# Second layer of a two-layer encoder: the softmax weights transposed by VectorE in 32x32 blocks and a trip through DRAM, in place of TensorE transposes

## The chip, the cores and the metric

The kernel runs on one core of a Trainium2 chip. The metric is the device time of one execution in microseconds; the kernel before ran three times, 1224.99, 1226.17 and 1229.44 us, median 1226.17. A core has five engines with a queue of instructions each, taken in order: TensorE (PE, matmuls; its weight loads are shown apart as PEld), VectorE (DVE), ScalarE (ACT), GpSimd (POOL) and SyncE (SP), which here issues nearly all DMAs. SBUF holds the working data, PSUM the results of matmuls.

## The reference, cut to what matters

x is 1024 positions of 1024 features, the memory 256 rows. Layer 0 has windowed and dense grouped-query attention, layer 1 differential attention (C: 6 heads of 64, value width 128); both have a cross-attention (X: 4 heads) into the memory, a SiLU gate, and an output projection that is added to x. Layer 1, which alone the change touches:

```python
def odd_layer(x, mem_n, table, norm_g, w_in, lq1, lk1, lq2, lk2, subln_g, w_mem_kv, w_out, lam_init):
    h = rmsnorm(x, norm_g)
    q1, q2, k1, k2, v, xq, gate = _split(h @ w_in, ODD_SPLITS)
    ...
    s = jnp.einsum("ibqhd,ibshd->ibhqs", qi, kk) * (D ** -0.5)         # i: the two maps
    p = jax.nn.softmax(s + rel_bias_lookup(table, rel)[None, None], axis=-1)
    w = p[0] - lam * p[1]
    y_c = jnp.einsum("bhqs,bshe->bqhe", w, v)                          # per block of 128 queries
    y_c = rmsnorm(y_c, subln_g) * (1.0 - lam_init)
    y_x = memory_cross_attention(xq, mem_n, w_mem_kv)
    y = jnp.concatenate([y_c, y_x], axis=-1) * jax.nn.silu(gate)
    return x + y @ w_out
```

## The kernel before

All matmuls take their data as fp32r, a rounded form of fp32. Where the precision is needed, a value is held as two such numbers, hi (the rounded value) and lo (what the rounding left), and a product is a sum of two or three products of these. To "split" is to make hi by a copy on ScalarE and lo by a subtraction.

**Steps.** Attention goes in steps, one for a head (or, in X, for all four heads) and a block of 128 queries: in layer 1 8 steps of X (steps 0 to 7) and 48 of C (steps 8 to 55, eight for each head). `run_steps` (L475) runs them as a software pipeline. In its round i it emits, in this order: `hop` of step i-1, `s1` of step i, projection products as filler (`jobs.pull`), `s3` (value product) of a pair of steps that is ready, `s2` (transposes and split) of the step 2 before, `finish` of step i, and more filler. The filler is the projections of the coming heads (`acc`, L329) or, late in the layer, the early part of the output projection (`pre`); `po` is its rest. The order that the program text gives is not the final one: a list scheduler in the framework places each engine's instructions when the program is built, by its own estimates, and the order of each engine's queue is then fixed. `tc.issue_after(x)` keeps an instruction behind x; `keep_in_program_order` (used by the change) pins a DMA in SP's queue where the text has it.

**One step of C.** `s1`: for the two maps the scores `sc` of 128 queries by 1024 keys in PSUM, one after the other product with the keys' hi part (L1505, four matmuls of 128x512) and lo part (L1514, four). VectorE then adds the position bias and takes the row minimum in one pass per map (L1520: `e` from `sc` and `toep`), and ScalarE takes the exp in place and its row sum (L1523). `finish`: two small VectorE operations (L1528, L1530) and the combine of the two maps into one weight matrix `e` (L1532). `hop`: `word_copy`, a DMA of `e` to `er`, SBUF to SBUF, 512 KB, which only changes its type. `s2` (`dense_s2`, L570): eight TensorE transposes of 128x128 into PSUM (`te`, L580), four a bank, and from each bank the split into `PT` (`split_to`: hi on ScalarE L347, lo on VectorE L348). In C, `finish` of step i is kept behind the split of step i-2 (`behind`). `s3`, for two steps at once and one round after their last split: the value product `oc` (L1545, L1547: 16 matmuls), then the normalisation (`ssqc`, `rbcc`) and the gate.

**One step of X** is alike with other shapes: scores `sx` (L543), minimum, exp, a scaling on ScalarE in `finish`, the same hop and `s2`, and the value product `ox` (L656).

**Rings.** PSUM has two places of 128x1024 (`ps_s`: `sc`, `sx` and `ox` in turn), two of 128x512 for `te` and other small results (`ps_t`), and two for `acc`, `pre` and `oc` (`ps_a`). `e` has 4 buffers, `er` 2 in layer 1, `PT` one per half. Weights of the projections come by DMA (`wr`), are cast by VectorE (`wh`, L241), and their lo part is subtracted on GpSimd (`wl`, L243); output weights likewise (`wos`, L270 and L271).

## Time and profile before

| | |
|---|---|
| time of the runs | 1224.99, 1226.17, 1229.44 us, median 1226.17 |
| span of the profiled execution | 1228.9 us, 2.7 above that median; no other time of that execution is given |
| mean granted TensorE clock | 0.996 |
| layer 1, first scores of X to last value product of C | about 640 to 1157 us |
| busy in one head of C (741 to 820 us): PE, DVE, ACT, POOL | 79.0, 55.1, 38.8, 23.7 of 79 us |
| DMA in the same stretch | share 0.48 of 16 engines, 154 GB/s |
| last scores of C; last value product ends; output projection begins | 1135.9; 1157.3; 1162.0 us |
| HBM | 87.7 MB read, 39.9 MB written |

How to read it: the profile names each instruction by the line of the program that made it, its engine, its output and inputs. Busy time of TensorE is counted from the start of a matmul to its modelled end, and matmuls overlap, so the mean time of one (0.40 us for 128x512) is longer than the distance of two that follow each other (0.23 us). An order of instructions that is quoted below is the built program's, without any time; names carry buffer numbers there, and what stands in brackets are the engines whose semaphores an instruction waits for (DMAHW: a DMA).

### The profile page before, as it was taken

To read this page: it belongs to the slowest core of one execution; us is meant where nothing else is said; L and a number is where in the kernel's file an instruction comes from. 1 tells how busy PE (TensorE), PEld (TensorE's weight loads), DVE (VectorE), ACT (ScalarE), POOL (GpSimd) and SP (SyncE) were. 2 spreads that over 40 slices of the span, in tenths; PEclk is the share of its full clock that TensorE was granted. 3 is DMA by queue.
4 is the path that set the end of the run, shared out by engine and by line. 5 is a ranking of instruction groups with operands and counts; after the bars stand their busy time and mean duration, and the time that the engine had idled before them with its cause. 6 is when DMAs were issued, how large, how long until landed. Compare 5 with 4: busy or idle time off the path is not lost.

```text
span 1228.9 us, 19560 instructions
## 1 busy us (share of the span) xinstructions
PE 1196.5 (97%) x6614; PEld 988.4 (80%) x6614; DVE 801.1 (65%) x1495; ACT 663.1 (54%) x1477; POOL 436.3 (36%) x414
## 2 busy tenths in 40 slices
PE   6999999999999999999999999999999999999997
PEld 5788888888888777888888777777787777777886
DVE  5547665377778878635365866766767767667544
ACT  6248754366667766636157744555545454445332
POOL 5023365366665455437112222333143231301100
PEclk9999999999999999999999999999999999999999
DMA  6664445545465565457645445355363452468354
GB/s 257 200 194 147 163 172 163 166 160 207 163 233 209 208 227 191 151 196 237 186 158 156 153 146 164 121 183 163 124 187 125 153 171 105 149 212 285 121 192 155
DMA packets 114304, 216.70 MB, mean 176 GB/s; under 512 B 13302, under 2 KB 47478, under 8 KB 114204
## 3 DMA queue, kind: packets, MB, share of 16 engines
q1 hardware_dynamic: 114060, 215.25, 52.5%
q8 instruction: 53, 0.87, 0.3%
q14 instruction: 47, 0.39, 0.1%
q10 hardware_dynamic: 144, 0.20, 0.0%
HBM read 87.71 MB, written 39.86 MB: 104 GB/s over the span
## 4 chain that ended last, share of the span: by engine, by line
PE 47%; DVE 2%; DMA 1%; issue 1%; ACT 1%; POOL 0%; POOLq 0%; SPq 0%; DVEq 0%; ACTq 0%
PE acc L329 24%; PE po L702 5%; PE oc L1545 3%; PE sc L1505 3%; PE te L580 3%; PE sc L1514 2%; PE pre L702 2%; PE oc L1547 2%; DMA wr<-in_w_in 1%; PE ssqc L1563 1%; PE ox L656 0%; PE rbcc L1576 0%; PE tv L439 0%; PE sx L543 0%; DVE e L1520 0%
## 5 line engine op out<-in xcount | busy, mean ns | idle before, releaser
L329 PE MATMUL acc<-h,wh 128*128 128x512 f32 x1536 | 499.5, 398 | 1.6 <-DVE h L351 0.8
L329 PEld LDWEIGHTS acc<-h,wh 128*128 128x128 f32 x1536 | 282.4, 188 | 65.7 <-issue 7.9
L329 PE MATMUL acc<-h,wl 128*128 128x512 f32 x768 | 303.8, 396 | 1.5 <-POOL wl L243 1.2
L243 POOL TENSOR_TENSOR wl<-wr,wh 128x512 fp32r<-128x512 f32 x94 | 124.8, 1329 | 286.3 <-DVE wh L241 155.0
L1523 ACT ACTIVATE e<-e,mn 128x1024 f32<-128x1024 f32 x96 | 110.0, 1148 | 117.0 <-DVE mn L1520 116.9
L329 PEld LDWEIGHTS acc<-h,wl 128*128 128x128 f32 x768 | 144.3, 188 | 34.9 <-issue 4.4
L1114 POOL TENSOR_TENSOR e<-e,rz 128x1024 f32<-128x1024 f32 x48 | 91.6, 1910 | 84.2 <-DVE rz L1113 57.8
L1520 DVE CUSTOM_DVE_ANT_0 e<-sc,toep 128x1024 f32<-128x1024 f32 x96 | 113.5, 1218 | 8.0 <-PE sc L1514 7.3
L580 PEld LDWEIGHTS te<-identr,er 128*128 128x128 f32 x896 | 92.2, 143 | 18.8 <-PE sa L543 2.2
L580 PE MATMUL te<-identr,er 128*128 128x128 f32 x896 | 99.9, 246 | 4.3 <-DVE O L1578 1.4
L348 DVE TENSOR_TENSOR PT<-te,PT 128x512 fp32r<-128x512 f32 x112 | 74.3, 687 | 42.8 <-ACT PT L347 39.2
L241 DVE CAST wh<-wr 128x512 fp32r<-128x512 f32 x112 | 58.2, 522 | 42.9 <-PE acc L329 17.3
L348 DVE TENSOR_TENSOR PTl<-te,PTh 128x512 fp32r<-128x512 f32 x112 | 74.0, 684 | 9.4 <-ACT PTh L347 8.9
L1545 PE MATMUL oc<-PT,v 128*128 128x512 f32 x192 | 69.8, 403 | 0.7 <-DVE ckl L1420 0.7
L1532 DVE SCALAR_TENSOR_TENSOR e<-e,mr 128x1024 f32<-128x1024 f32 x48 | 66.3, 1381 | 1.5
L347 ACT CAST PT<-te 128x512 fp32r<-128x512 f32 x112 | 62.7, 589 | 7.2 <-PE te L580 6.7
L347 ACT CAST PTh<-te 128x512 fp32r<-128x512 f32 x112 | 62.2, 586 | 7.9 <-PE te L580 7.1
L702 PE MATMUL po<-woh,yh 128*128 128x512 f32 (+1 forms) x172 | 65.7, 382 | 0.0
L702 PE MATMUL po<-woh,yl 128*128 128x512 f32 (+1 forms) x172 | 65.5, 381 | 0.0
L702 PE MATMUL po<-wol,yh 128*128 128x512 f32 (+1 forms) x172 | 65.3, 380 | 0.0
L1105 DVE TENSOR_REDUCE mn<-sb 128x1 f32<-128x1024 f32 x48 | 58.3, 1216 | 7.0 <-PE sb L543 6.6
L350 ACT ACTIVATE yh<-yr 128x256 fp32r<-128x256 f32 (+2 forms) x56 | 24.0, 447 | 66.2 <-DMA yr<-ysc 37.5
(211 smaller groups left out, 2358.7 us busy)
## 6 DMA issues: line engine op xcount, KB each, us to landing
er<-e SPq DMA_DIRECT2D x112, 512.0 KB, 3.0
wr<-in_w_in SPq DMA_DIRECT2D x96, 256.0 KB, 3.0
ysc<-gy SPq DMA_DIRECT2D x16, 512.0 KB, 2.7
cq<-sg SPq DMA_DIRECT2D x64, 128.0 KB, 2.5
ck<-sg SPq DMA_DIRECT2D x48, 128.0 KB, 2.3
er<-e SPq DMA_DIRECT2D x12, 384.5 KB, 2.6
xpsc<-xh SPq DMA_DIRECT2D x18, 256.0 KB, 2.6
xr<-xpsc SPq DMA_DIRECT2D x9, 512.0 KB, 3.6
```

Of the source, the lines that this page charges most:

```text
L243: (nc.vector if fast else nc.gpsimd).tensor_tensor(out=lo, in0=raw, in1=hi, op=ALU.subtract)
L329: lastmm[0] = nc.tensor.matmul(acc, a, b[:, k, c0:c0 + n], start=(i == 0), stop=(i == 23))
L347: nc.scalar.copy(hi, src)
L348: return nc.vector.tensor_tensor(out=lo, in0=src, in1=hi, op=ALU.subtract)
L580: nc.tensor.transpose(to[:, i * P:(i + 1) * P], e[0][:, k * P:(k + 1) * P], idt)
L702: lastmm[0] = nc.tensor.matmul(acc, a, b, start=(start and n == 0), stop=(stop and n == 2))
L1105: nc.vector.tensor_reduce(out=mn, in_=Sp, op=ALU.min, axis=AX.X)
L1114: nc.gpsimd.tensor_tensor(out=et, in0=et, in1=rz.to_broadcast([P, 1024]), op=ALU.mult)
L1520: nc.vector.tensor_tensor_reduce(out=et, in0=Sp, in1=toeps[h][:, w0:w0 + 1024], scale=1.0, scalar=BIG, op0=ALU.add, op1=ALU.min, accum_out ...
L1523: nc.scalar.activation(et, et, AF.Exp, bias=mn[:, m:m + 1], scale=-1.0, accum_out=z[:, m:m + 1])
L1532: nc.vector.scalar_tensor_tensor(out=es[0], in0=es[1], scalar=c, in1=es[0], op0=ALU.mult, op1=ALU.add)
L1545: nc.tensor.matmul(acc, V[:, kt, 0, :], ph.both[:, kt, :], start=(kt == 0), stop=(kt == 7), skip_group_check=True)
```

## The change

In layer 1 the TensorE transposes are gone. `finish` of a step ends with one VectorE operation that transposes each 32x32 block of the 128x1024 weight matrix within its group of 32 partitions (`blocks_turned`, L577). A matrix is transposed when the blocks have also changed places between partition groups, and that is done by DMAs: `turned_out` writes the matrix to one of three DRAM buffers (512 KB, one a step), and `turned_in`, once for a pair of steps, reads it back with four DMAs, one for each group of 32 partitions (256 KB each, in runs of 1 KB), into a single `er` buffer. All these DMAs are pinned in SP's order. `turned_s2` then splits from SBUF: hi by a ScalarE copy (L611, two a step, each kept behind the last exp that the text has emitted, `M.exped`), lo by a subtraction on GpSimd (L612, two a step of 128x4x128) instead of VectorE. Both steps of a pair split in the same round, the second step's third, and the value product comes one round later than before. `finish` is no longer kept behind a split. In `run_steps` the pinned DMAs stand behind the round's first filler, the DMA of the fetch two rounds after its step. Layer 0 is as it was.

By count, for 56 steps: TensorE −448 transposes; VectorE −112 subtractions, +56 block transposes; ScalarE 112 copies as before, now from SBUF; GpSimd +112 subtractions; SP −56 copies, +56 writes, +112 reads.

```diff
...
     def dma(out, in_, eng=None):
         if out.dtype == F32R and in_.dtype == F32R:
             out, in_ = out.bitcast(F32), in_.bitcast(F32)
-        (eng or nc.sync).dma_start(out=out, in_=in_)
+        return (eng or nc.sync).dma_start(out=out, in_=in_)
...
+    turn_d = [dr.tile([2, P, S], F32, name="turn_d%d" % i) for i in range(3)]
...
         p2 = p3 = 0
         finish = None
         for i in range(n + LAG + 1):
-            behind = None
             if jobs is not None:
                 jobs.step = i
             if hooks:
                 hooks(i)
-            if 0 < i <= n and steps[i - 1].hop:
+            if 0 < i <= n and steps[i - 1].hop and not steps[i - 1].fetch:
                 steps[i - 1].hop()
             if i < n:
                 if steps[i].need:
...
                 jobs.pull(f - f // 2 - two)
                 if hooks:
                     hooks(-1)
+            if 0 < i <= n and steps[i - 1].fetch:
+                steps[i - 1].hop()
+            if 1 < i <= n + 1 and steps[i - 2].fetch:
+                steps[i - 2].fetch()
             for q in list(posts):
                 q.pop(0)()
                 if not q:
                     posts.remove(q)
+            while p3 < n and p3 + steps[p3].lag + 1 <= i and steps[p3].s3 is None and steps[p3].fetch:
+                p3 += 1
             if p3 < n and p3 + steps[p3].lag + 1 <= i:
                 st, p3 = steps[p3], p3 + 1
                 if st.s3 is not None:
...
                     if st.s3b is not None:
                         jobs.pull(two)
                         st.s3b()
-            if p2 < n and p2 + steps[p2].lag <= i:
-                behind = steps[p2].s2()
+            while p2 < n and p2 + steps[p2].lag <= i:
+                steps[p2].s2()
                 p2 += 1
             if finish:
-                with (tc.issue_after(behind.ins) if behind is not None else nullcontext()):
-                    finish()
+                finish()
                 finish = None
             if jobs is not None:
                 jobs.pull(f // 2)
...
         need3 = ()
         lag = 2
         hop = None
+        fetch = None
         s3 = None
         fill = 0
 
...
             e[0] = t
         return f
 
-    def dense_s2(M, e, st, late=False):
+    def blocks_turned(dst, src):
+        nc.vector.transpose(out=dst.rearrange("p (c k j) -> p k c j", c=4, k=8),
+                            in_=src.rearrange("p (k c j) -> p k c j", c=4, k=8))
+
+    def turned_out(M, e, st):
+        def f():
+            if st.sub == 0:
+                M.nturn = (M.nturn + 1) % len(turn_d)
+            st.grp["turn"] = turn_d[M.nturn]
+            tc.keep_in_program_order(dma(st.grp["turn"][st.sub], e[0]))
+        return f
+
+    def turned_in(M, st):
+        def f():
+            if st.sub == 0:
+                return
+            t = M.at.tile([P, 2, 4, 256], F32, tag="er", name="er", bufs=1)
+            src = st.grp["turn"].rearrange("s (g i) (c x) -> c i (s g) x", g=4, c=4)
+            for c in range(4):
+                d = dma(t[32 * c:32 * c + 32].rearrange("p s g x -> p (s g) x"), src[c])
+                tc.keep_in_program_order(d)
+            st.grp["er"] = t
+        return f
+
+    def turned_s2(st):
+        def f():
+            if st.sub == 0:
+                st.grp["pt"] = new_pt(M)
+            h, lo = st.grp["pt"]
+            er = st.grp["er"][:, st.sub].rearrange("p g (k j) -> p k g j", k=8)
+            for j in range(2):
+                ks = slice(4 * j, 4 * j + 4)
+                o = slice(st.sub * P, st.sub * P + P)
+                hv, lv = (t[:, ks, o].rearrange("p k (g j) -> p k g j", g=4) for t in (h, lo))
+                with tc.issue_after(M.exped.ins):
+                    nc.scalar.copy(hv, er[:, ks])
+                nc.gpsimd.tensor_tensor(out=lv, in0=er[:, ks], in1=hv, op=ALU.subtract)
+        return f
+
+    def turn_pairs(M, e, st):
+        st.lag = 4 - st.sub
+        st.hop = turned_out(M, e, st)
+        st.fetch = turned_in(M, st)
+        st.s2 = turned_s2(st)
+
+    def dense_s2(M, e, st):
         def f():
             if st.sub == 0:
                 st.grp["pt"] = new_pt(M)
...
                     nc.tensor.transpose(to[:, i * P:(i + 1) * P], e[0][:, k * P:(k + 1) * P], idt)
                 Tv = T.rearrange("p (k c) -> p k c", k=4)
                 o = slice(st.sub * P, st.sub * P + P)
-                r = split_to(h[:, 4 * j:4 * j + 4, o], lo[:, 4 * j:4 * j + 4, o], Tv)
-            return r if late else None
+                split_to(h[:, 4 * j:4 * j + 4, o], lo[:, 4 * j:4 * j + 4, o], Tv)
         return f
 
     def mem_jobs(M, l, memT, X):
...
                 ev = et.rearrange("p (h m) -> p h m", h=4)
                 z = stat("z4", 4)
                 for h in range(4):
-                    nc.scalar.activation(ev[:, h, :], Sp[:, h, :], AF.Exp, bias=mn[:, h:h + 1],
-                                         scale=-1.0, accum_out=z[:, h:h + 1])
+                    M.exped = nc.scalar.activation(ev[:, h, :], Sp[:, h, :], AF.Exp, bias=mn[:, h:h + 1],
+                                                   scale=-1.0, accum_out=z[:, h:h + 1])
                 def finish():
                     rz = stat("rz4", 4)
                     nc.vector.reciprocal(rz, z)
                     for h in range(4):
                         nc.scalar.activation(ev[:, h, :], ev[:, h, :], AF.Copy, scale=rz[:, h:h + 1])
                     e[0] = et
+                    if M.wide:
+                        e[0] = new_e(M)
+                        blocks_turned(e[0], et)
                 return finish
             st.s1 = s1
-            st.hop = word_copy(M, e)
-            st.s2 = dense_s2(M, e, st)
+            if M.wide:
+                turn_pairs(M, e, st)
+            else:
+                st.hop = word_copy(M, e)
+                st.s2 = dense_s2(M, e, st)
             if st.sub == 1:
                 def s3(qb=qb, grp=grp):
                     v = X["v"]
...
                     nc.vector.tensor_tensor_reduce(out=et, in0=Sp, in1=toeps[h][:, w0:w0 + 1024], scale=1.0,
                                                    scalar=BIG, op0=ALU.add, op1=ALU.min,
                                                    accum_out=mn[:, m:m + 1])
-                    nc.scalar.activation(et, et, AF.Exp, bias=mn[:, m:m + 1], scale=-1.0,
-                                         accum_out=z[:, m:m + 1])
+                    M.exped = nc.scalar.activation(et, et, AF.Exp, bias=mn[:, m:m + 1], scale=-1.0,
+                                                   accum_out=z[:, m:m + 1])
                     es.append(et)
                 def finish():
                     rz = stat("rz")
...
                                                    op0=ALU.mult, op1=ALU.mult)
                     nc.vector.scalar_tensor_tensor(out=es[0], in0=es[1], scalar=c, in1=es[0],
                                                    op0=ALU.mult, op1=ALU.add)
-                    e[0] = es[0]
+                    blocks_turned(es[1], es[0])
+                    e[0] = es[1]
                 return finish
             st.s1 = s1
-            st.hop = word_copy(M, e)
-            st.s2 = dense_s2(M, e, st, True)
+            turn_pairs(M, e, st)
             if st.sub == 1:
                 def s3(h=h, qb=qb, grp=grp):
                     ph, pl_ = grp["pt"]
```

Three places of the built orders. **First place, TensorE, where X passes into C.** Steps 8 and 9 are C's first two; `ox` is X's value product. Of the kernel before:

```order
L656 MATMUL ox_7873<-PT_7774,xv1_6898 128x256 [waits DVE_49]
...
L656 MATMUL ox_7873<-PT_7775,xv1_6898 128x256 x4
L1505 MATMUL sc_7930<-ck0_7466,cq_7703 128x512 [waits DVE_49]
L1505 MATMUL sc_7930<-ck0_7466,cq_7703 128x512
L329 MATMUL acc_7959<-h_6290,wh_7650 128x512
L329 MATMUL acc_7959<-h_6289,wl_7651 128x512
...
L580 MATMUL te_7976<-identr_74,er_7853 128x128 [waits DMAHW4_49,DVE_49]
...
L1505 MATMUL sc_7931<-ck1_7467,cq_7706 128x512 [waits DVE_49,PE_49,Activation_49]
```

And now:

```order
L1570 MATMUL sc_7813<-ckl_7457,cq_7676 128x512
L1561 MATMUL sc_7850<-ck0_7455,cq_7673 128x512 [waits DVE_49]
...
L1561 MATMUL sc_7851<-ck1_7456,cq_7676 128x512 [waits DVE_49]
...
L1570 MATMUL sc_7850<-ckl_7457,cq_7673 128x512
L1570 MATMUL sc_7851<-ckl_7457,cq_7676 128x512
L712 MATMUL ox_7902<-PT_7829,xv1_6901 128x256 [waits DVE_49,Activation_49]
L1561 MATMUL sc_7954<-ck0_7455,cq_7673 128x512 [waits DVE_49]
L712 MATMUL ox_7902<-PT_7829,xv1_6901 128x256 [waits Pool_49]
L712 MATMUL ox_7902<-PT_7829,xv1_6901 128x256 x2
L712 MATMUL ox_7902<-PT_7830,xv1_6901 128x256 [waits Activation_49]
```

Before, 17 projection products and the eight transposes of a step stood between the first half of step 9's scores (sc_7930) and its second map (sc_7931); now all of step 9 (sc_7850 and sc_7851) follows step 8 at once, and X's value product of its third pair of steps stands behind it.

**Second place, the same passage on VectorE, now.** L1576 is the bias and minimum of one map, L1588 the combine, L577 the block transpose; wh is a cast of weights:

```order
L1576 ISA e_7822,mn2_7811<-sc_7812,toep_7422 128x1024 [waits DMAHW1_49,DVE_49,PE_49]
...
L1576 ISA e_7825,mn2_7811<-sc_7813,toep_7422 128x1024 [waits DMAHW2_49,PE_49]
...
L1576 ISA e_7860,mn2_7849<-sc_7850,toep_7422 128x1024 [waits DMAHW7_49,PE_49]
...
L1584 RECIPROCAL rz_7839<-mn_7810 128x1 [waits Activation_49]
L1586 SCALAR_TENSOR_TENSOR mr_7841<-mn_7810,misc_84,rz_7839 128x1 [waits DVE_49]
L1588 SCALAR_TENSOR_TENSOR e_7822<-e_7825,mr_7841,e_7822 128x1024 [waits DVE_49]
L1612 SCALAR_TENSOR_TENSOR es_8280<-mn_7810 128x2 [waits Activation_49]
L577 STREAM_TRANSPOSE e_7825<-e_7822 128x8x4x32 [waits DVE_49]
L1576 ISA e_7863,mn2_7849<-sc_7851,toep_7422 128x1024 [waits DVE_49,PE_49]
```

The second map of step 9 (sc_7851) stands behind the combine and the block transpose of step 8. And on GpSimd at the same place, PT being lo, wl a weight's lo part:

```order
L612 TENSOR_TENSOR PT_7829<-er_7768,PT_7829 128x4x128 [waits DMAHW1_49,DMAHW2_49,DMAHW0_49,DMAHW3_49,PE_49,Activation_49]
L612 TENSOR_TENSOR PT_7830<-er_7768,PT_7830 128x4x128 [waits PE_49,Activation_49]
L612 TENSOR_TENSOR PT_7829<-er_7768,PT_7829 128x4x128 [waits Activation_49]
L612 TENSOR_TENSOR PT_7830<-er_7768,PT_7830 128x4x128 [waits Activation_49]
L244 TENSOR_TENSOR wl_7869<-wr_7866,wh_7868 128x512 [waits DMAHW5_49,DVE_49]
L244 TENSOR_TENSOR wl_7875<-wr_7872,wh_7874 128x512 [waits DMAHW6_49,DVE_49]
```

Four subtractions in a row stand ahead of the weights, where before there was no such subtraction on GpSimd.

**Third place, TensorE at the last steps.** Now, steps 53, 54 and 55 (sc_12066, sc_12155, sc_12230) with two small products between:

```order
L1561 MATMUL sc_12066<-ck0_11262,cq_11590 128x512 [waits DVE_49]
...
L1561 MATMUL sc_12067<-ck1_11263,cq_11593 128x512 [waits DVE_49]
...
L1570 MATMUL sc_12067<-ckl_11264,cq_11593 128x512
L1632 MATMUL rbcc_12100<-ident_69,rz2_12030 128x128 [waits Pool_49]
...
L1561 MATMUL sc_12155<-ck0_11262,cq_11590 128x512 [waits DVE_49,PE_49]
...
L1561 MATMUL sc_12156<-ck1_11263,cq_11593 128x512 [waits DVE_49,PE_49]
...
L1570 MATMUL sc_12156<-ckl_11264,cq_11593 128x512
L1561 MATMUL sc_12230<-ck0_11262,cq_11590 128x512 [waits DVE_49]
...
L758 MATMUL pre_11966<-woh_11781,yh_11959 128x512 [waits DMAHW0_49,Activation_49]
```

Before, 20 products of `pre` stood between steps 53 and 54, and 16 with a value product between 54 and 55, with eight transposes each time.

2 lines of the change are left out of this document (1 added, 1 removed).

## The prediction, made before the changed kernel had run

> **What bounds the kernel now.** First the page: the busy line says that TensorE works nearly all the time.
>
> ```profile
> span 1228.9 us, 19560 instructions
> PE 1196.5 (97%) x6614; PEld 988.4 (80%) x6614; DVE 801.1 (65%) x1495; ACT 663.1 (54%) x1477; POOL 436.3 (36%) x414
> ```
>
> The change is in layer 1 only, so next the busy times by stretch (after the range: length, then PE, PEld, DVE, ACT, POOL busy with counts, clock, DMA share, GB/s): the passage from layer 1's cross-attention (X) to its differential attention (C), one head of C, and head 4 to 5.
>
> ```profile
> 690.00:741.00 51.00, 49.74 (x261) 38.64 (x260) 36.65 (x70) 27.44 (x55) 15.07 (x15) 1.00 0.48 154
> 741.00:820.00 79.00, 79.00 (x419) 62.73 (x418) 55.05 (x99) 38.76 (x79) 23.66 (x25) 1.00 0.48 154
> 1057.00:1136.00 79.00, 79.00 (x422) 62.08 (x421) 56.13 (x104) 39.96 (x82) 9.89 (x10) 1.00 0.67 225
> ```
>
> TensorE is the only engine without slack: 79 of 79 us, against 55 on VectorE and 24 on GpSimd. Even the passage loses only 1.3 us, and the waits of TensorE in it say to what:
>
> ```profile
> PE oc L1545 <- DVE ckl L1420: 0.7, 1, 0.7
> PE ox L656 <- DVE mn L1520: 0.4, 1, 0.4
> PE tv L439 <- DVE PT L348: 0.2, 1, 0.2
> ```
>
> So TensorE work removed there is time removed, as long as TensorE stays fed. The chain that ended last shows what a step's work takes on it:
>
> ```profile
> 747.09 0.37 PE te L580 x4
> 747.46 0.54 PE acc L329 x2
> 748.00 0.29 PE te L580 x4
> 748.29 5.09 PE acc L329 x22
> 753.38 0.91 PE sc L1505 x4
> 754.28 0.66 PE sc L1514 x4
> ...
> 759.02 0.23 PE oc L1545
> 759.25 0.12 PE oc L1547
> ```
>
> **What goes.** Eight transposes of a step take 0.37 + 0.29 = 0.66 us of the chain; 56 steps (8 of X, 48 of C): 56 × 0.66 = 37 us. That is the whole possible gain. The groups of instructions price the rest (busy, mean ns):
>
> ```profile
> L1523 ACT ACTIVATE e<-e,mn 128x1024 f32<-128x1024 f32 x96 | 110.0, 1148 | 117.0 <-DVE mn L1520 116.9
> L1520 DVE CUSTOM_DVE_ANT_0 e<-sc,toep 128x1024 f32<-128x1024 f32 x96 | 113.5, 1218 | 8.0 <-PE sc L1514 7.3
> L348 DVE TENSOR_TENSOR PT<-te,PT 128x512 fp32r<-128x512 f32 x112 | 74.3, 687 | 42.8 <-ACT PT L347 39.2
> L1532 DVE SCALAR_TENSOR_TENSOR e<-e,mr 128x1024 f32<-128x1024 f32 x48 | 66.3, 1381 | 1.5
> L347 ACT CAST PT<-te 128x512 fp32r<-128x512 f32 x112 | 62.7, 589 | 7.2 <-PE te L580 6.7
> L241 DVE CAST wh<-wr 128x512 fp32r<-128x512 f32 x112 | 58.2, 522 | 42.9 <-PE acc L329 17.3
> L1105 DVE TENSOR_REDUCE mn<-sb 128x1 f32<-128x1024 f32 x48 | 58.3, 1216 | 7.0 <-PE sb L543 6.6
> L243 POOL TENSOR_TENSOR wl<-wr,wh 128x512 fp32r<-128x512 f32 x94 | 124.8, 1329 | 286.3 <-DVE wh L241 155.0
> L1114 POOL TENSOR_TENSOR e<-e,rz 128x1024 f32<-128x1024 f32 x48 | 91.6, 1910 | 84.2 <-DVE rz L1113 57.8
> ```
>
> A GpSimd group after 690 us, and the DMA issues (KB each, us to landing):
>
> ```profile
> L271 POOL TENSOR_TENSOR wos<-wor,wos 128x256 fp32r<-128x256 f32 x31 | 26.7, 862 | 48.9 <-ACT wos L270 48.5
> er<-e SPq DMA_DIRECT2D x112, 512.0 KB, 3.0
> wr<-in_w_in SPq DMA_DIRECT2D x96, 256.0 KB, 3.0
> ysc<-gy SPq DMA_DIRECT2D x16, 512.0 KB, 2.7
> ```
>
> The slowest combine in the timeline, beside a GpSimd subtraction, and all combines from 741 to 1136 (ns):
>
> ```profile
> 870.45 2.34 DVE L1532 SCALAR_TENSOR_TENSOR e<-e,mr 128x1024 f32<-128x1024 f32 x1
> 870.42 1.29 POOL L243 TENSOR_TENSOR wl<-wr,wh 128x512 fp32r<-128x512 f32 x1 [1.85 <-PE acc L329]
> L1532 DVE SCALAR_TENSOR_TENSOR e<-e,mr x40: 1283/1285/2344, 741.4 to 1127.4; 128x1024 f32<-128x1024 f32 x40
> ```
>
> **What comes, by engine.** VectorE loses two subtractions a step (2 × 0.69 = 1.37) and gains one block transpose of 128x1024, which no row shows. Bounds: two casts of 128x512, 2 × 0.52 = 1.04, below; the slowest pass over 128x1024 (the combine of 2.34) above. I take 1.22, the one-input pass over 128x1024 (the reduction, L1105). VectorE's load stays near 55 us a head. [...]
>
> GpSimd gains the subtractions: two a step of 128x512. The nearest row is the 128x512 subtraction at 1.33; bounds 0.95 (half of the 128x1024 at 1.91) and 2 × 0.86 = 1.72 (the 128x256, L271). A head of 8 steps adds 16 × 1.33 = 21 us to GpSimd's 24: 45 of 79, not a bound by itself.
>
> ScalarE's copies stay 112 and keep 0.59. DMA: a step's 512 KB copy (3.0) becomes 512 KB out (the row to DRAM, 2.7) and half of four 256 KB fetches (3.0 each, together perhaps 4 to 6). They have two steps of about 79/8 = 10 us until the split, at a DMA share of 0.48: hidden, at nothing. Without this cover each of 28 pairs would pay its 4 to 6. The pinned fetch waits on SP for the single er buffer, which GpSimd's fourth subtraction frees; weight loads (wr) stand behind it.
>
> **Where a wait comes.** A step's chain is now reduction, exp, combine, block transpose, DRAM, copy, and for a pair of steps four subtractions in a row; the value product stands one step later than before to cover it. VectorE takes its instructions in order, so a second reduction that stands behind combine and transpose waits for the exp too, and score banks come free late. In the new order TensorE has its projection products mostly between two steps' scores, as before; but at three places steps stand one behind the other with little between. There I follow the chain with the rows above (reduction 1.22, exp 1.15, combine 1.38, transpose 1.22, copy 0.59, subtraction 1.33, a step's scores 1.57).
>
> *Passage X to C (steps 8 to 14).* Scores of 8 end at 0. Reductions 1.2 and 2.4; scores of 9 go in as banks come free and end at 3.5. VectorE: map 0 of step 9 to 4.7, combine 8 to 6.1, transpose to 7.3, map 1 of step 9 to 8.5; ScalarE: its exp to 9.7, and only then the first copy of X's pair 4/5, 10.3; GpSimd: third subtraction 10.3 + 3 × 1.33 = 14.3, fourth 15.6. X's value product (ox) is next on TensorE after 3.5 and needs these: 11.5 us idle, with the little between third and fourth. The next ox (pair 6/7) stands directly behind step 11's scores; its copies stand behind an exp again: 1.2 + 1.15 + 0.59 + 3 × 1.33 + 0.86 (an output-weight subtraction between) = 7.8, so about 8. Steps 13 and 14 adjoin: map 1 of 14 waits for a reduction behind combine and transpose, 1.2 + 1.4 + 1.2 + 1.2 = 5.0 less what TensorE does meanwhile: 4. Sum 23.5, less the 1.3 of before: **22**.
>
> *Start of head 5 (steps 48 to 51).* Scores of 49, 50, 51 adjoin. Map 1 of 50 waits 5.0 as above less its own 0.5: 4.8; map 0 of 51 for combine and transpose of 49 and a reduction, 1.4 + 1.2 + 1.2 = 3.9; the value product before them and a weight's low part, both on GpSimd's queue, 2 × 1.33 = 2.7 and 2.1 (a subtraction of 1.33 with its cast of 0.52 and the rest of one ahead). Sum **13.5**.
>
> *Last steps (53 to 55).* The same, 5.3 at step 54 and 4.2 at 55, and the value product of pair 48/49 meets three subtractions: 1.2 + 1.15 + 0.6 + 4.0 against 3.3 of TensorE work, 3.6. Sum **13**.
>
> Elsewhere two pairs of steps adjoin (30 and 31, 38 and 39) with about 1 us each: **2.5**. At the end the chain behind step 55 (two reductions 2.4, exp 1.15, combine 1.4, transpose 1.2, out 2.7, fetch 5, copy 0.6, four subtractions 5.3: 19.8) lies beside 58 output products of 0.23 and two value products of 8 × (0.23 + 0.12) in the new order, 19: 0 to 1, taken as **0**.
>
> Sum against the profile's own time: 1228.9 − 37 + 22 + 13.5 + 13 + 2.5 = 1243. The span lies 2.7 above the median 1226.17 of the runs shown, so the forecast is **1240 us**, 1.1% slower. Transpose at 2.34: seven of them lie on these chains, +8; at 1.04: −1. Subtraction at 0.95 or 1.72: some sixteen on the chains, −6 or +6. Chains a quarter shorter or longer give ±13: own range 1230 to 1256.
>
> **The rivals.**
> (1) *The gain is kept.* Adjoining rows need not be idle time: if exps and transposes run earlier than I chain them, the three places cost under 20. 1226 − 37 + 0 to 20 = 1190 to 1209. For it: 79 of 79 busy today, VectorE with 24 us free a head. Against: four subtractions of 1.33 ahead of a product that is next on TensorE. 0.13.
> (2) *Only the passage costs*, because there alone X's own split hangs behind C's exps; 1226 − 37 + 22 + 2.5 = 1214. 0.17.
> (3) *Gain and stalls cancel*: 31 to 43 lost, 1220 to 1232. 0.12.
> (4) *Slower still, GpSimd against VectorE.* The combine that met a GpSimd subtraction took 2.34 against a median of 1.285: 1.06 more. With GpSimd nearly doubled, one such meeting in each of 24 pairs of C that reaches TensorE costs 24 × 1.06 = 25: 1240 + 25 = 1265. It decides only where the reduction behind the combine is what TensorE waits for; in a head with 24 us of slack it isn't. 0.10. [...]
>
> **How the numbers follow.** The forecast has the remaining 0.48. A measurement of this kernel tells about 0.5%, 6 us, from no change. Faster: (1) and (2), 0.30; same: (3) and the forecast's lower edge, 0.14; slower: 0.56. Leaving out most of (1) and the far half of (4), the range for 8 in 10 is 1205 to 1262.
>
> **What would show it.** No transposes on TensorE in layer 1, and its busy time near 1160. Gaps on TensorE at the passage (about 11 and 8 us, released by GpSimd's PT), at head 5's start and in the last 3 steps (released by VectorE's mn), with full stretches elsewhere. A block transpose of 1.0 to 1.4 and a subtraction near 1.33. I am wrong if the gaps sum to under 31 us, if they lie in the steady heads, or if the fetch from DRAM, not GpSimd, releases the copies.

## The result, and the profile after

The changed kernel took 1378.65 us (1378.42 to 1379.47, 4 runs), the kernel before 1227.08 (1224.99 to 1229.44, 4 runs): a ratio of 1.1241, 95% interval 1.1223 to 1.1259. It is 12% slower; the prediction was 1240 with a range of 1205 to 1262.

From the page after: its first lines, the row of the granted clock in 40 slices, the rows of instructions that answer to those of before, and its DMA issues:

```profile
span 1376.7 us, 18789 instructions
PE 1220.1 (89%) x6166; PEld 982.4 (71%) x6166; DVE 831.6 (60%) x1439; ACT 663.3 (48%) x1477; POOL 593.8 (43%) x526
...
PEclk9999999999999999999967899999898899787899
...
L612 POOL TENSOR_TENSOR PT<-er,PT 128x512 fp32r<-128x512 f32 x112 | 153.6, 1400 | 76.7 <-ACT PT L611 74.5
L577 DVE STREAM_TRANSPOSE e<-e 128x1024 f32<-128x1024 f32 x56 | 69.5, 1242 | 10.2 <-ACT e L688 9.2
L1588 DVE SCALAR_TENSOR_TENSOR e<-e,mr 128x1024 f32<-128x1024 f32 x48 | 70.2, 1462 | 1.3
...
turn_d<-e SPq DMA_DIRECT2D x56, 512.0 KB, 4.0
er<-turn_d SPq DMA_DIRECT2D x112, 256.0 KB, 5.6
wr<-in_w_in SPq DMA_DIRECT2D x96, 256.0 KB, 3.0
```

448 matmuls are gone, and TensorE is busy for longer than before (1220.1 against 1196.5). The clock row says why: from the middle on the granted clock is no longer full. By stretches of the layer (length, TensorE's busy time, its granted clock, DMA share and GB/s), with two stretches of 10 us at their worst:

```profile
640.00:690.00 50.00, 41.71 (x201) 0.93 0.58 157
690.00:760.00 70.00, 45.27 (x163) 0.68 0.39 118
760.00:860.00 100.00, 88.79 (x412) 0.97 0.64 182
860.00:960.00 100.00, 85.66 (x365) 0.90 0.59 173
960.00:1060.00 100.00, 87.06 (x373) 0.90 0.60 176
1060.00:1160.00 100.00, 82.77 (x365) 0.93 0.57 167
1160.00:1260.00 100.00, 77.78 (x312) 0.81 0.56 176
1260.00:1310.00 50.00, 32.49 (x133) 0.80 0.59 175
sum 670.00, PE 541.53; mean PE 67.69
...
700.00:710.00 10.00, 2.26 (x7) 0.50 0.13 52
1230.00:1240.00 10.00, 4.24 (x10) 0.50 0.00 0
```

The same layer before:

```profile
640.00:1160.00 520.00, 517.22 (x2766) 1.00 0.49 160
```

In the 670 us from 640 to 1310 TensorE is now busy 541.5 and idle 128.5. Before, it was busy 517 of 520 us; less the 37 of the transposes that is 480 of work. So the work took 541.5 − 480 = 61 us longer at the lower clock, and idle time grew by about 125: −37 + 61 + 125 = +149, against a span that is 147.8 longer. The waits of TensorE in this part (us in total, times, longest):

```profile
PE oc L1601 <- POOL PT L612: 40.3, 11, 7.5
PE sc L1561 <- DVE mn L1576: 32.7, 16, 4.0
PE ox L712 <- ACT PT L611: 12.3, 2, 8.5
PE ox L712 <- POOL PT L612: 8.6, 7, 3.0
PE sc L1561 <- DMA cq<-sg: 6.9, 3, 2.8
PE acc L330 <- DVE ckl L1476: 6.7, 1, 6.7
PE tv L440 <- ACT vraw L435: 4.4, 4, 1.3
```

The time from one head's first reduction (bias and minimum) to the next one's, read from VectorE's timeline, shows that the loss is in every head and not only at the three places of the prediction (us):

| kernel | first reduction of C | length of heads 0 to 4 | last reduction of C |
|---|---|---|---|
| before | 678.6 | 76.4, 78.7, 78.7, 80.4, 78.7 | 1138.9 |
| after | 691.3 | 109.9, 85.3, 97.6, 95.5, 94.9 | 1263.5 |

Heads 1 to 4 together are 57 us longer. TensorE idles 49 us in them, where it idled 1.4 before; and its work there, 294 us without the transposes, takes 324.

### The profile page after: what moved, and what is told of

Read it like the earlier page. It is cut to its first block, busy times and chain, and to the rows that moved or that the text cites. A ratio compares the mean times of both kernels' runs of the same rounds, so it can differ in the third digit from the quotient of the medians.

```text
span 1376.7 us, 18789 instructions
## 1 busy us (share of the span) xinstructions
PE 1220.1 (89%) x6166; PEld 982.4 (71%) x6166; DVE 831.6 (60%) x1439; ACT 663.3 (48%) x1477; POOL 593.8 (43%) x526
## 5 line engine op out<-in xcount | busy, mean ns | idle before, releaser
L330 PE MATMUL acc<-h,wh 128*128 128x512 f32 x1536 | 505.8, 404 | 15.9 <-DVE ckl L1476 6.7
L330 PEld LDWEIGHTS acc<-h,wh 128*128 128x128 f32 x1536 | 289.5, 192 | 85.7 <-issue 9.5
L612 POOL TENSOR_TENSOR PT<-er,PT 128x512 fp32r<-128x512 f32 x112 | 153.6, 1400 | 76.7 <-ACT PT L611 74.5
L1576 DVE CUSTOM_DVE_ANT_0 e<-sc,toep 128x1024 f32<-128x1024 f32 x96 | 114.4, 1216 | 44.4 <-PE sc L1570 41.2
L1601 PE MATMUL oc<-PT,v 128*128 128x512 f32 x192 | 89.8, 492 | 40.6 <-POOL PT L612 40.3
L242 DVE CAST wh<-wr 128x512 fp32r<-128x512 f32 x112 | 70.0, 632 | 73.3 <-DMA wr<-in_w_in 42.3
L1561 PE MATMUL sc<-ck,cq 128*128 128x512 f32 x192 | 67.0, 452 | 45.2 <-DVE mn L1576 32.7
L1601 PEld LDWEIGHTS oc<-PT,v 128*128 128x128 f32 x192 | 46.0, 239 | 58.2 <-POOL PT L612 45.2
L232 POOL TENSOR_TENSOR rz<-z,nhalf 128x2 f32<-128x2 f32 x24 | 21.2, 883 | 140.8 <-ACT z L1623 134.0
L1561 PEld LDWEIGHTS sc<-ck,cq 128*128 128x128 f32 x192 | 36.6, 209 | 62.8 <-DVE mn L1576 38.2
L577 DVE STREAM_TRANSPOSE e<-e 128x1024 f32<-128x1024 f32 x56 | 69.5, 1242 | 10.2 <-ACT e L688 9.2
L1588 DVE SCALAR_TENSOR_TENSOR e<-e,mr 128x1024 f32<-128x1024 f32 x48 | 70.2, 1462 | 1.3
```

What stands on the lines that cost most here:

```text
L242: nc.vector.tensor_copy(hi, raw)
L330: lastmm[0] = nc.tensor.matmul(acc, a, b[:, k, c0:c0 + n], start=(i == 0), stop=(i == 23))
L612: nc.gpsimd.tensor_tensor(out=lv, in0=er[:, ks], in1=hv, op=ALU.subtract)
L1561: full = nc.tensor.matmul(Sps[m][:, c], C[h][(m, qb // 4)][:, qc], C[h]["k"][m][:, c], start=True, stop=False)
L1576: nc.vector.tensor_tensor_reduce(out=et, in0=Sp, in1=toeps[h][:, w0:w0 + 1024], scale=1.0, scalar=BIG, op0=ALU.add, op1=ALU.min, accum_out ...
L1588: nc.vector.scalar_tensor_tensor(out=es[0], in0=es[1], scalar=c, in1=es[0], op0=ALU.mult, op1=ALU.add)
```

## The experiments

Times are of one run each; the kernel before, beside them, took 1224.9 to 1227.0. Runs of one kernel agree within 0.4%, about 5 us, so only differences well above that are read.

**Moving the lo subtraction back to VectorE.**

```diff
-                nc.gpsimd.tensor_tensor(out=lv, in0=er[:, ks], in1=hv, op=ALU.subtract)
+                nc.vector.tensor_tensor(out=lv, in0=er[:, ks], in1=hv, op=ALU.subtract)
```

> One edit to the changed kernel (1378.7 us): the lo subtraction of the split runs on VectorE instead of GpSimd. Split theory (TensorE waits for copies that stand behind the exps and then for four GpSimd subtractions in a row, and each wait also costs clock): the 49 us of waits that GpSimd's PT releases go, with their share of the clock loss (63 x 49/128 = 24): about 1305, 1285 to 1330. VectorE theory (the block transpose makes VectorE late with the reductions): VectorE gets 2 x 0.69 us more a step, so slower, 1385 to 1410. DRAM theory (write and fetch land too late): no change, 1372 to 1385.

1352.4 us. The 40 us that C's value product waited for the lo parts of PT fell to 10, but it now waited for other things, and these four rows add up to 41 again:

```profile
PE oc L1601 <- DVE sg L352: 13.6, 3, 4.5
PE oc L1601 <- DVE PT L612: 10.1, 5, 3.1
PE oc L1601 <- DVE ckl L1476: 8.8, 3, 3.7
PE oc L1601 <- ACT yh L351: 8.3, 1, 8.3
```

GpSimd's four subtractions are the last link of many waits, but taking them away gives back 26 us, not 73.

**Copies not kept behind the exps.**

```diff
-                with tc.issue_after(M.exped.ins):
-                    nc.scalar.copy(hv, er[:, ks])
+                nc.scalar.copy(hv, er[:, ks])
```

> One edit to the changed kernel: ScalarE's hi copies are no longer kept behind the last exp. Split theory: the copies start about two exps (2.3 us) earlier at each pair, 28 x 2.3 = 64 us at most of which a third to all is waited for today: 1310 to 1355. VectorE theory and DRAM theory: no change, 1372 to 1385.

1377.8 us: no change. The constraint was not what placed them there; TensorE's waits for PT, released by GpSimd (41.6 us) and by ScalarE (12.3 us), are as in the changed kernel (40.3 and 12.3), and in the built order of ScalarE nearly every copy stands where it stood: the scheduler puts them behind the exps by itself. So this run moved almost nothing, and says little of what the place behind the exps costs.

**A fetch that doesn't wait for its own pair's write to land.**

```diff
...
-            src = st.grp["turn"].rearrange("s (g i) (c x) -> c i (s g) x", g=4, c=4)
+            src = (M.turned or st.grp["turn"]).rearrange("s (g i) (c x) -> c i (s g) x", g=4, c=4)
...
+            M.turned = st.grp["turn"]
```

> One edit to the changed kernel: the fetch reads the DRAM buffer that the pair of steps before wrote, so it never waits for the block transpose or for the write of its own pair (4.0 us) to land; all instructions and DMAs stay. The weights in the value product are then those of the pair before. DRAM theory: most of the waits go, 1290 to 1330. Split theory: the copies wait for exps and GpSimd, not for data, except at the last three pairs (17 us of waits there): 1355 to 1380. VectorE theory: as the split theory.

1386.9 us, 8 more than the changed kernel. The wait for a pair's write to land is not what costs. The fetch still stands in SP's queue behind the write of a later step, and that write waits for its block transpose (SP's waits for L577 are 47 us in the changed kernel and 30 here, where the line is L578), so this run does not clear the rest of the chain.

**More work for TensorE.**

```diff
                     V = C[h]["v"]
+                    warm = ps_t("warm")
+                    for i in range(16):
+                        nc.tensor.matmul(warm, V[:, 0, 0, :], V[:, 0:2].rearrange("p t i d -> p (t i d)"),
+                                         start=True, stop=True)
                     acc = ps_a("oc")
```

> One edit to the changed kernel: 16 matmuls of 128x512 whose result nobody reads stand directly ahead of each of C's 24 value products: 24 x 16 x 0.23 = 88 us of additional TensorE work. The waits ahead of these products are 40 us today, so at a clock that does not depend on waiting the time rises by 48 or more: 1425 to 1440. If the halved clock is a consequence of the waits, the clock comes back where a wait is filled, and 25 to 45 us of the rise are given back: 1380 to 1400, with a mean granted clock above 0.95 instead of 0.937.

1362.7 us: with 88 us of additional products the kernel is 16 us faster, at a mean clock of 0.976 instead of 0.937. Its stretches in the middle:

```profile
860.00:960.00 100.00, 99.48 (x472) 1.00 0.65 193
960.00:1060.00 100.00, 94.97 (x446) 1.00 0.57 169
```

Where the waits are filled the clock is full (1.00 in both stretches, 0.90 in the changed kernel). TensorE's busy time rose by 49 us (1220.1 to 1269.0) for 88 us of additional products, so the rest of its work took 39 us less: the clock loss follows from the waits and is worth tens of us. That is more than was expected of this run. A part of the gain can be the order, which was built anew: in heads 2 and 3 one pair of adjoining steps went apart.

**The removal alone.** The kernel before, transposes of layer 1 left out, the split straight from the copied weights:

```diff
...
-                T = ps_t("te")
...
+                if M.wide:
+                    T = e[0].bitcast(F32)[:, 4 * j * P:4 * j * P + 4 * P]
...
```

> The kernel before with its 448 TensorE transposes of layer 1 left out: the split reads the copied weights straight from SBUF on ScalarE and VectorE, everything else stays, so the value products take weights that are not transposed. Route theory (the gain of 37 us is there, the new route through VectorE, DRAM and GpSimd loses it): 1227 - 37 = 1190, 1185 to 1205. Filler theory (without the transposes TensorE runs dry at each wait and its clock halves on any route): 1215 to 1260.

1190.0 us: 36 us less than the kernel before beside it (1225.9). The whole gain is to be had when nothing new comes in its place, and TensorE does not run dry without the transposes (granted clock 0.999).

**VectorE's and GpSimd's additional work alone,** each added to the steps of C in the kernel before, with unused results. The block transpose:

```diff
+                    nc.vector.transpose(out=es[1].rearrange("p (c k j) -> p k c j", c=4, k=8),
+                                        in_=es[0].rearrange("p (k c j) -> p k c j", c=4, k=8))
```

> The kernel before with VectorE's block transpose of each step of C added (48 x 1.25 = 60 us of VectorE work), its result unused. If VectorE's load and its in-order queue are what makes the changed kernel slow, most of the loss in the heads shows here too: 1260 to 1320. If VectorE's slack covers it: 1227 to 1235.

1227.5 us. The two subtractions:

```diff
+                    for j in range(2):
+                        o = slice(512 * j, 512 * j + 512)
+                        nc.gpsimd.tensor_tensor(out=es[1][:, o], in0=es[0][:, o], in1=es[1][:, o], op=ALU.subtract)
```

> The kernel before with two GpSimd subtractions of 128x512 on SBUF added to each step of C (96 x 1.33 = 128 us of GpSimd work), results unused. [...] If only the wait of the value product on it matters, which is absent here: 1227 to 1240.

1225.6 us. Against 1225.9 neither load costs more than runs of one kernel differ.

**X back on TensorE.** In the changed kernel, X's steps get the copy and `dense_s2` of before, with one er buffer and the split one step after.

> The changed kernel with X's 8 steps back on TensorE transposes (one er buffer, split one step after), C as changed. First scores of C came 12.7 us later than before and head 0 of C took 110 us where the later heads take about 95. If the passage is a cost of its own: 12.7 + 14 + 2 less 8 x 0.66 = about 1355, 1345 to 1362. If the waits of the passage are only moved into head 0: 1370 to 1385.

1338.6 us, 40 less. First scores of C at 677.9 and head 0 in 86.6 us, but heads 2 to 4 still take 95 each. So X's trip and the passage are a cost of their own, larger than the 22 that the forecast gave the passage, and less than a third of the loss.

**Everything but the trip.** The kernel of the removal alone, with the block transpose in the chain and GpSimd's subtraction:

```diff
...
+                    nc.scalar.copy(hv, er[:, ks])
+                    r = nc.gpsimd.tensor_tensor(out=lv, in0=er[:, ks], in1=hv, op=ALU.subtract)
...
-                    e[0] = es[0]
+                    nc.vector.transpose(out=es[1].rearrange("p (c k j) -> p k c j", c=4, k=8),
+                                        in_=es[0].rearrange("p (k c j) -> p k c j", c=4, k=8))
+                    e[0] = es[1]
...
```

> The kernel before without its TensorE transposes of layer 1 (1190), plus the changed kernel's block transpose in each step's chain and its lo subtraction on GpSimd; the 512 KB copy from SBUF to SBUF and the pipeline (split two steps later, step by step) stay those of before, so the 32x32 blocks never change places between partition groups. Trip theory (the two DMAs in series through DRAM, with the pair-wise split that they bring, are the cause): 1190 to 1210. If block transpose and GpSimd's subtractions in the chain cost by themselves: 1230 to 1300.

1203.7 us, within the 1190 to 1210 of the trip theory. Its page:

```profile
span 1201.6 us, 18635 instructions
PE 1155.9 (96%) x6166; PEld 947.5 (79%) x6166; DVE 819.6 (68%) x1439; ACT 663.6 (55%) x1477; POOL 597.2 (50%) x526
```

It has the changed kernel's 6166 matmuls, and they are busy for 1155.9 us instead of 1220.1: 64 of the 175 us between the two spans are busy time at a lower clock (0.937 against 0.998), 111 are idle time. All of it comes with the trip through DRAM and what was changed in the pipeline and in the built order for it.

**No pins; step by step; value product later.** Each in the changed kernel. First, fetches and writes without their pins:

```diff
-            tc.keep_in_program_order(dma(st.grp["turn"][st.sub], e[0]))
+            dma(st.grp["turn"][st.sub], e[0])
...
-                tc.keep_in_program_order(d)
```

> The changed kernel without the pins: the scheduler places the writes and fetches in SP's queue. If pinned DMAs that wait hold back the loads behind them (weights, keys, queries) and so TensorE: 1280 to 1340. If the order of SP doesn't matter: 1365 to 1390.

1371.0 us, 8 less. Then the trip step by step, with the lo part on VectorE:

```diff
...
+            t = M.at.tile([P, 4, 256], F32, tag="er", name="er", bufs=2)
+            src = st.grp["turn"][st.sub].rearrange("(g i) (c x) -> c i g x", g=4, c=4)
...
+                nc.vector.tensor_tensor(out=lv, in0=er[:, ks], in1=hv, op=ALU.subtract)
...
-        st.lag = 4 - st.sub
+        st.lag = 3
...
```

> The changed kernel with the trip through DRAM kept, but step by step: write and fetch of each step at the start of a round and not pinned, two er buffers of half the size, split three steps later for each step, lo on VectorE, copies free of the exps. If the pair-wise split (four copies and four subtractions at once, one er buffer) is the cause: 1190 to 1250. If it is the length of the trip itself: 1310 to 1360, near the 1352 with lo on VectorE.

1378.7 us. Last, the value product one round later, by the same condition in three places:

```diff
...
-            if p3 < n and p3 + steps[p3].lag + 1 <= i:
+            if p3 < n and p3 + steps[p3].lag + 1 + 1 * (steps[p3].fetch is not None) <= i:
```

> The changed kernel with the value product one more round behind its split. If the split comes too late for its value product (40 us of waits in C, with their share of the clock): 1300 to 1335. If the next split then waits for the value product to release the weights' only buffer, so that the loop is as long as before: 1360 to 1390.

1378.9 us. Each time other waits took the place of those that went; with the value product later the first of the list is the projection's wait for its weights:

```profile
PE acc L330 <- POOL wl L244: 36.0, 15, 6.1
PE sc L1561 <- DVE mn L1576: 22.2, 14, 3.9
PE pre L758 <- ACT yh L351: 12.8, 2, 12.0
```

**The trip as load that nobody waits for.** The kernel of no_dram_trip; each step's weights are also written to DRAM, and each pair has four more DMAs that copy them within DRAM as the fetch does:

```diff
...
+    def trip_out(st):
...
+        tc.keep_in_program_order(dma(turn_d[M.nturn][st.sub], st.kept))
+
+    def trip_in(st):
+        if st.sub:
+            src = turn_d[st.grp["turn"]].rearrange("s (g i) (c x) -> c i (s g) x", g=4, c=4)
+            for c in range(4):
+                tc.keep_in_program_order(dma(back_d[st.grp["turn"]][32 * c:32 * c + 32].rearrange("p s g x -> p (s g) x"), src[c]))
...
```

> The kernel of no_dram_trip (1203.7 us) with the changed kernel's DRAM traffic added as load: each step's write to DRAM and each pair's four fetches (into DRAM again, pinned as in the changed kernel), which no engine waits for. Load theory (the 168 more DMAs in SP's queue, pinned, and 58 MB more traffic delay the weights, keys and queries behind them): 1260 to 1340. Lateness theory (only that the split waits for the trip): 1203 to 1215.

1399.9 us: 196 more than without, and more than the changed kernel itself, which has 56 copies fewer. No engine uses what these DMAs bring, so the trip does its harm without anyone waiting for its data. The writes still wait for the step's weights and hold their `e` buffer; load_without_waits below takes that away.

**Two fetch buffers.**

```diff
-            t = M.at.tile([P, 2, 4, 256], F32, tag="er", name="er", bufs=1)
+            t = M.at.tile([P, 2, 4, 256], F32, tag="er", name="er", bufs=2)
...
+        if h:
+            toeps[h] = toeps[0]
+            return
...
-                    sq = M.pl.tile([P, 256], F32, tag="sq", name="sqc", bufs=2)
+                    sq = M.pl.tile([P, 256], F32, tag="sq", name="sqc", bufs=1)
...
```

> The changed kernel with two er buffers instead of one; for the space, all heads use head 0's bias table (7 table loads left out) and one sq buffer. One-buffer theory: a pair takes 23.5 us because fetch, wait for the exps and copies' start (12.6), copies and subtractions (7.5) and the way to the next fetch (3.4) stand in a ring through the only buffer; with two, heads fall from 95 to about 80 to 85: 1290 to 1330. Load theory and late-split theory: 1360 to 1385.

1396.4 us, not faster, although SP's waits for the subtractions that free the buffer (L612) fall from 59.9 us to 0.6. The ring through the single buffer falls as a cause. ScalarE's waits ahead of the squares that go into the lone sq buffer don't grow (13.5 us, and 15.3 in the changed kernel), so that edit hides no gain.

**The exchange without DRAM,** 16 DMAs of 32 KB a step from SBUF to SBUF, on SP (below) or on SP and ScalarE in turn (with `nc.scalar if (c + g) % 2 else None` in place of `None`), in the kernel of no_dram_trip:

```diff
...
+                for c in range(4):
+                    for g in range(4):
+                        dma(t.bitcast(F32)[32 * c:32 * c + 32, 256 * g:256 * g + 256],
+                            e[0][32 * g:32 * g + 32, 256 * c:256 * c + 256], None)
...
```

> A right result without DRAM: as no_dram_trip, but the copy from SBUF to SBUF is 16 DMAs of 32 KB, each moving one 32-partition group's blocks to another, all on SP. At the 0.33 to 0.6 us that SP takes for one issue, 5.3 to 9.6 us of a step of 9.4: if SP's queue is what counts (load theory), 1260 to 1400; if not, 1203 to 1225.

> As exchange_by_sp with every second DMA on ScalarE's queue: SP 2.6 to 4.8 us a step. Load theory: better than exchange_by_sp by at least 30 us, unless ScalarE, which then waits for the block transpose ahead of its exps, takes its place; 1205 to 1300.

1497.5 and 1366.5 us. The same bytes and DMAs cost 131 us less when half of them are issued elsewhere. In the first, the rows of SP's timeline from 1000 to 1100 add up to 94 of 100 us, and VectorE waits 49.6 us for weights (19.3 in the second), which fits a full issuing queue that brings weights late; the built orders of the two differ too, so the 131 us are not shown to be the queue's alone.

**The load without its waits, and the trip on another queue.** First, the added DMAs of trip_as_load_only copy rows of x within DRAM:

```diff
-        tc.keep_in_program_order(dma(turn_d[M.nturn][st.sub], st.kept))
+        tc.keep_in_program_order(dma(turn_d[M.nturn][st.sub], x_d[0:P, :]))
...
-            src = turn_d[st.grp["turn"]].rearrange("s (g i) (c x) -> c i (s g) x", g=4, c=4)
+            src = x_d[0:2 * P, :].rearrange("(s p) x -> s p x", s=2).rearrange("s (g i) (c x) -> c i (s g) x", g=4, c=4)
```

> As trip_as_load_only (1399.9 us), but the added writes and fetches copy rows of the input x within DRAM, so SP never waits for a step's data ahead of them; count, sizes and place in the queue stay. If SP waits at the added DMAs and holds what stands behind them: 1203 to 1240. If their number and traffic alone are enough (issue time on SP, transfers): 1340 to 1410.

1398.6 us, as with the waits. Then the changed kernel with write and fetches issued by ScalarE, not pinned:

> The changed kernel with the trip's DMAs (write and four fetches) issued by ScalarE instead of SP, not pinned; traffic as before. If SP's queue is what the trip clogs: 1200 to 1290. If the DMA engines' traffic is what counts: 1350 to 1385. If ScalarE's queue, which then stands at the trip's waits ahead of exps and copies, is no better a place: 1290 to 1350.

1380.8 us, as on SP. So the loss doesn't need SP's waits for the trip's data, and it doesn't go when the trip leaves SP's queue (ScalarE's queue then has the trip's waits). That the DMAs are added is enough. By what way they cost is less plain. What the landing times say of the traffic, in no_dram_trip:

```profile
er<-e SPq DMA_DIRECT2D x112, 512.0 KB, 3.2
wr<-in_w_in SPq DMA_DIRECT2D x96, 256.0 KB, 2.9
cq<-sg SPq DMA_DIRECT2D x64, 128.0 KB, 2.9
ck<-sg SPq DMA_DIRECT2D x48, 128.0 KB, 2.6
```

and in load_without_waits:

```profile
er<-e SPq DMA_DIRECT2D x112, 512.0 KB, 3.4
wr<-in_w_in SPq DMA_DIRECT2D x96, 256.0 KB, 3.1
cq<-sg SPq DMA_DIRECT2D x64, 128.0 KB, 4.1
ck<-sg SPq DMA_DIRECT2D x48, 128.0 KB, 4.6
...
PE sc L1540 <- DVE mn L1555: 41.4, 22, 3.9
PE acc L331 <- POOL wl L245: 24.6, 14, 3.5
PE acc L331 <- DVE wh L243: 12.5, 6, 2.9
```

Weights and copies land 0.2 us later by the median, keys and queries 1.2 to 2.0. The last three rows are TensorE's largest waits there: for VectorE's reductions and for weights, not for those keys and queries. VectorE's own waits for weight DMAs hardly grew (17.1 us from 690 to 1310, and 15.1 in no_dram_trip). What else the added DMAs changed is the built order: the scheduler, which counts them by its own estimates, placed all engines' instructions anew. The number of projection products on TensorE from the last score product of one step to the first of the next, in the built order of head 2 (the first number: from the last step of head 1):

| kernel | products between the scores of adjacent steps |
|---|---|
| before | 32, 24, 16, 21, 24, 24, 24, 24 |
| no_dram_trip | 32, 24, 16, 24, 24, 24, 24, 24 |
| after | 24, 24, 0, 24, 24, 24, 24, 0 |
| trip_as_load_only, load_without_waits | 34, 9, 4, 9, 24, 0, 24, 0 |
| trip_on_act_queue | 48, 0, 16, 24, 24, 0, 0, 0 |

The kernels that are near 1200 have an even order, the slow ones an uneven one, though no engine uses what the added DMAs of load_without_waits bring.

The heads of the changed kernel show the order apart from the traffic. Head 1 has an even order there (64, 24, 16, 24, 24, 24, 24, 24), heads 2 and 3 both have the row of the table, and each of the three has 8 writes and 16 fetches of the trip:

| head, after | us | TensorE busy | granted clock | DMA share | GB/s |
|---|---|---|---|---|---|
| 1 | 85.3 | 76.3 | 0.96 | 0.58 | 174 |
| 2 | 97.6 | 83.9 | 0.88 | 0.59 | 170 |
| 3 | 95.5 | 82.7 | 0.89 | 0.58 | 172 |

At the same traffic the uneven order goes with 10 to 12 us more a head, and with the lower clock; head 1, with its even order, still takes 10 more than the 75.3 of head 1 in no_dram_trip. The heads differ in the output weights that they load, too, so this is no proof, but the rebuilt order is probably a large part of the loss. How the 195 us divide between the transfers and the order stays open: no run had the trip's DMAs in the order of the kernel without them.

## Why the prediction was wrong, point by point

**The gain: right.** 56 × 0.66 = 37 us; 36 measured with the removal alone.

**The durations: right.** Block transpose 1.22 forecast, 1.242 measured; subtraction 1.33 forecast, 1.400 in the mean (median 1.292).

**"Hidden, at nothing" for the DMAs: the step that failed.** It compared the trip's length with the two steps until the split. The length was near enough (4.0 out and 5.6 for a fetch, against 2.7 and 4 to 6), and not waiting for the write to land gains nothing (fetch_of_pair_before). But 56 writes and 112 fetches that are merely added cost 196 us (trip_as_load_only) to a kernel that stands at 1203.7 without them. The prediction had no term for what more DMAs do to everything else, in the queues and in the order that the scheduler builds around them; which of these two it is stays open in part, as said above.

**"Elsewhere 2.5": wrong, and with it the three places.** The waits were sized well where the chains were followed: TensorE idles 24.7 us from 690 to 760, where the passage was given 23.5, and the first wait of X's value product was forecast at 11.5 and is 8.45, 2.98 and 0.19 in the timeline:

```profile
704.57 0.58 PE L712 MATMUL ox<-PT,xv 128*128 128x256 f32 x1 [8.45 <-ACT PT L611]
708.56 1.22 PE L712 MATMUL ox<-PT,xv 128*128 128x256 f32 x4 [2.98 <-POOL PT L612]
709.97 2.72 PE L712 MATMUL ox<-PT,xv 128*128 128x256 f32 x11 [0.19 <-POOL PT L612]
```

But the same chain (reduction behind combine and block transpose, exp, copies, four subtractions) stands in every pair of steps, and in heads 2 to 4, which the sum had at 74 us, TensorE waits in the middle of full stretches of filler too: the 49 us of idle time in heads 1 to 4 stand against this 2.5. The prediction had named waits in the steady heads as a sign that it is wrong. One such place, from the issue of a pair's fetch over ScalarE's exp and copies to GpSimd and TensorE:

```profile
853.41 2.36 SPq L175 DMA_DIRECT2D er<-turn_d  x4
866.27 1.14 ACT L1579 ACTIVATE e<-e,mn 128x1024 f32<-128x1024 f32 x1
867.40 2.17 ACT L611 CAST PT<-er 128x512 fp32r<-128x512 f32 x4
868.45 1.70 POOL L1637 TENSOR_TENSOR gy<-O,gy 128x256 f32<-128x256 f32 x1 [0.60 <-DVE O L1634]
870.11 5.12 POOL L612 TENSOR_TENSOR PT<-er,PT 128x512 fp32r<-128x512 f32 x4
874.05 0.69 PE L1601 MATMUL oc<-PT,v 128*128 128x512 f32 x1 [4.38 <-POOL PT L612]
```

The copies came 14 us after the fetch's issue, behind the exps of later steps, though a fetch lands in 5.6 by the median. The last steps were forecast at 13 and the end at 0; the list of waits from 1260 on has 17.0 us in three waits of value products for L612 alone. The 23 us by which the stretch from the last reduction to the end grew are that and the clock. Two slips in the sum for head 5 change little: 5.0 less 0.5 is 4.5 and not 4.8, and 1.4 + 1.2 + 1.2 is 3.8 and not 3.9.

**The clock: no term at all.** A wait was priced at its length. The clock falls with it: 61 to 64 us of the loss are matmuls at a lower clock, which adds about half to the 111 to 125 us of idle time. The granted clock is 0.50 at 700 to 710, around a wait of 8.45 us, and 1.00 from 860 to 1060 where products_ahead_of_oc fills the waits (0.90 there in the changed kernel). Heads 2 and 3, whose longest wait is 4.4 us, stand at 0.88 and 0.89; head 1, with the same longest wait, stands at 0.96. How long a wait must be before the clock falls is not shown here.

**The rivals.** (1) and (2), a gain, and (3), no change, fall for the kernel as it is; that only the passage costs is refuted by x_by_tensore, which still takes 1338.6. (4) named the right sign and the wrong cause: GpSimd's added work beside VectorE's costs nothing that can be told from the differences of runs (before_and_pool_subtractions, 1225.6 us against 1225.9), and the slowest combine of the changed kernel takes 2.29 us, against 2.34 before.

Of the versions here that compute what the reference does, none is faster than the kernel before by more than its runs differ.

## What to carry to other kernels

Before an exchange of engine work for DMAs, try the DMAs alone, with nobody waiting for them. Here that showed the whole loss (1203.7 to 1399.9 us) on the kernel of no_dram_trip; it was not tried on the kernel before. In a kernel that a scheduler orders, more DMAs are a change of every queue, so a sum of durations that gives them no cost of their own says little about them: count the products between adjoining steps in the new order, head by head. And on a TensorE that was 97% busy a gap cost more than its length, since the products after it ran at down to half the clock (0.50 granted from 700 to 710 us): 111 us of idle time came with 64 us of slower work, so such waits are priced here at about one and a half times their length.

## What was not expected of the hardware

A kernel with 384 additional matmuls of 128x512 ran 16 us faster than without them (1362.7 against 1378.65), while the clock rose from 0.937 to 0.976. With half of 896 small DMAs moved from SP to ScalarE's queue the kernel took 131 us less (1497.5 to 1366.5), while moving the 168 larger ones of the trip saved nothing (1378.65 to 1380.8).
